# Cutting the weight blocks of a fused hybrid block into their two fp32r parts in two halves, while recurrences run

## The chip, the cores and the metric

The kernel runs on one core of a Trainium2 chip. The metric is the device time of one execution in microseconds, median over the runs shown. The core has TensorE (PE, matmuls and transposes, with its weight loads listed apart as PEld), VectorE (DVE), ScalarE (ACT), GpSimd (POOL) and SyncE (SP), which issues the DMAs of the weights. The engines run side by side, each in its own order, and wait for one another by semaphores.

## The reference

The block takes 256 tokens and 16 meta tokens in front of them, width 2048, in fp32. One input projection gives the inputs of three recurrences and of three gates:

```python
h = jnp.concatenate([meta, x], axis=1)                  # 272 x 2048
xn = rmsnorm(h, norm_g[l])
(a_q, ..., g_a, g_b, g_c) = split_cols(xn @ w_in[l])    # w_in: 2048 x 18568
y_a = hgrn2_mixer(a_q, a_f, a_i, a_z, ...)              # A: 8 heads of 128 x 128
y_b = mlstm_mixer(b_q, b_k, b_v, b_o, b_ig, b_fg, b_z, ...)   # B: 4 heads
y_c = rwkv7_mixer(c_r, c_k, c_v, c_wd, c_ad, c_z, ...)  # C: 16 heads of 64 x 64
merged = (jax.nn.sigmoid(g_a) * (y_a @ w_br[l, 0])
          + jax.nn.sigmoid(g_b) * (y_b @ w_br[l, 1])
          + jax.nn.sigmoid(g_c) * (y_c @ w_br[l, 2]))
h = h + merged @ w_out[l]
return rmsnorm(h, final_norm_g)[:, N_META:]
```

Each recurrence goes over the tokens in chunks and carries a state from one chunk to the next. C solves a triangular system in each chunk.

## The kernel before

**Products.** Every large product is made of three matmuls in fp32r, a rounded form of fp32: with x = xH + xL and w = wh + wl, where the H and h parts are the rounded values and the L and l parts what is left, the kernel sums xH·wh, xL·wh and xH·wl. The parts of the activations are made once. The parts of the weights are made as the weights arrive.

**The weight stream.** `Stream` (its `cut` is the function that the change edits) brings the weights in 372 units of 128 partitions. A unit is 4 x 256 elements (four k tiles of 128 rows, 256 columns) in the first part of the run, 2 x 512 in the gates and the end, and 4 x 128 for four units at the start. `load` issues the unit's DMA into `raw` (4 buffers). `cut` makes two instructions: ACT copies `raw` into `wh`, which rounds it, and DVE subtracts `wh` from `raw` into `wl`; each has 3 buffers. `next` hands the oldest pair to the products. A unit feeds 24 matmuls that write PSUM tiles called `gp` (12 of 512 columns in the gates). In `unit`, the 24 go through one column tile of 128 and then the other; in each, k runs from 0 to 3 and each k has its three matmuls.

**What runs when.** The program first normalizes and transposes x (tiles `xt`, then `xH` and `xL`), then takes the projection column block by column block: groups b0, c1, b1, c2, a0, a1, c3, a2, a3, with c0 first, then the gates of B, C and A with their products with `w_br`, then `w_out`. The recurrence of a group is a generator. `Order` keeps a clock for each engine by a list of prices; after the matmuls of a column tile `pump` lets a generator go on if its next step would be ready by those clocks. The prices are taken from every DVE and ACT instruction that is written, through the helper `Priced`, whose line 127 therefore stands in the profile for all of them (matmuls are on line 186, transposes on line 193). After that the tile framework's scheduler sets the order of each engine's queue, so the order in the code isn't the order on the engines. The steps of a generator that the profile names are these. For A: `aE`, `aW`, `aQ`, `aK` (decays and their products), `ATT` (scores), `avt` (values), `aY`, `aYH`, `aYL` (output norm), all in PSUM tiles called `bank`. For C, in PSUM tiles called `cbank`: `BK` and `RA` (inputs of the chunks), `SC` (scores), `LU`, `LV`, `Ltmp` and `LT` (the triangular solve, a row of DVE instructions for a whole group), then for each of five chunks `UV,SC`, `cX,Vm`, `UV,BT` and `SC,UV`, `RA,Zs`, each needing the one before, and at the end `cSH`, `cSL` (the norm of the group's output).

**The end of the last C recurrence.** `l_setup`, called ahead of the first gate block, closes the pool of C when its last recurrence has ended, and opens the pool `late`, which holds among others the tiles `yHB` and `yLB` (the parts of B's output) of the block after it. The matmuls of the first gate block itself (8 units) read only `xH`, `xL` and the weights. `x_again`, after the last block of gate B, sets `late["rp"]`.

Of the kernel before, what the change touches and what calls it, by code (L numbers as in the profile page):

```python
# [9 lines left out]
F32 = mybir.dt.float32  # L10
# [4 lines left out]
ALU = mybir.AluOpType  # L15
# [135 lines left out]
def kernel(  # L151
# [29 lines left out]
    od = Order()  # L181
    V = Priced(nc.vector, "dve", od, tc)
    S = Priced(nc.scalar, "act", od, tc)
# [148 lines left out]
    class Stream:  # L332
# [18 lines left out]
        def cut(self):  # L351
            if not self.raw:
                return
            raw, uk, m = self.raw.pop(0)
            if self.extra and len(self.todo) + len(self.raw) < len(self.extra):
                h, l = self.extra.pop(0)
            else:
                h = wts.tile([P, uk, max(m, 256)], F32R, name="wh", tag="wh", bufs=3)
                l = wts.tile([P, uk, max(m, 256)], F32R, name="wl", tag="wl", bufs=3)
            saved, od.ready = od.ready, 0.0  # L360
            S.copy(out=h[:, :, 0:m], in_=raw[:, :, 0:m])
            od.ready = 0.0
            V.tensor_tensor(out=l[:, :, 0:m], in0=raw[:, :, 0:m], in1=h[:, :, 0:m].bitcast(F32), op=ALU.subtract)
            od.ready = saved
            self.split.append((h, l))

        def next(self):
# [4 lines left out]
                self.load()  # L372
            return self.split.pop(0)

    ws = Stream()

    def unit(h, l, u, kts, ps, aH, aL, t0, n, js):
# [955 lines left out]

    late = {}
    WB = 512
    TK = 2

# [222 lines left out]
    for u in range(KT // UK):  # L1562
        h, l = ws.next()
        unit(h, l, u, KT, gw[0][:, 0:T], xH, xL, 0, T, slice(0, P))
        h, l = ws.next()
# [103 lines left out]
    for n, (c0, m) in enumerate(outs):  # L1669
        ps = [gps.tile([P, 512], F32, name="gp", tag="g") for _ in range(2)]  # L1670
        us = KT * m // 1024
        if n < len(outs) - 1:
            for u in range(us):
                h, l = ws.next()
# [55 lines left out]
```

## Time and profile before

| | before |
|---|---|
| time, median of 3 runs | 1229.77 us (1229.72 to 1230.2) |
| the profiled execution's own time | 1229.33 us |
| its span | 1227.6 us |
| TensorE busy | 1208.1 us, 98% |
| VectorE busy | 879.2 us, 72% |
| ScalarE busy | 665.0 us, 54% |
| HBM read | 202.19 MB, 168 GB/s over the span |

The span runs from the first to the last instruction that the profile counts. The busy times are sums over the whole of it and include stages with different limits. A matmul counts as busy until its result is written, and matmuls overlap, so that their durations don't add up to the time that a row of them takes; that is read from their starts.

### The profile page before, as it was taken

How to read it: one execution, taken by the hardware profiler on the slowest of the kernel's cores; microseconds unless marked ns; L12 is line 12 of the kernel's file. 1: busy time of each engine (PE TensorE's matmuls, PEld its weight loads, DVE VectorE, ACT ScalarE, POOL GpSimd, SP SyncE). 2: the span in 40 equal slices, each digit the busy share in tenths (PEclk: the TensorE clock that was granted, in tenths of full speed). 3: DMA queues.
4: the chain of work that ended last, by engine and by line, in shares of the span. 5: the costliest groups of instructions: out<-in, count | busy, mean ns of one | idle time of the engine just before them, and what ended most of it. 6: DMA issues, size and time to landing. Idle time of an engine off the chain costs nothing.

```text
span 1227.6 us, 23061 instructions
## 1 busy us (share of the span) xinstructions
PE 1208.1 (98%) x9224; PEld 1104.2 (90%) x9224; DVE 879.2 (72%) x1491; ACT 665.0 (54%) x1032; POOL 57.0 (5%) x167
## 2 busy tenths in 40 slices
PE   8999999999999999999999999999999999999997
PEld 8999999999999999999999988888888888888887
DVE  6688996697975889995889986644555565556554
ACT  6765455663445764766664657544444444445444
POOL 3100001000051000010000000000000000000000
PEclk9999999999999999999999999999999999999999
DMA  8645564465563554463554454666766676665663
GB/s 254 184 138 166 155 172 130 129 183 155 155 171 104 158 165 137 140 170 105 162 163 142 139 164 153 190 188 189 226 197 193 191 225 200 191 193 172 193 197 121
DMA packets 172996, 207.43 MB, mean 169 GB/s; under 512 B 22331, under 2 KB 127160, under 8 KB 172488
## 3 DMA queue, kind: packets, MB, share of 16 engines
q1 hardware_dynamic: 171688, 202.21, 56.2%
q0 software_dynamic: 880, 3.22, 0.8%
q8 instruction: 72, 1.18, 0.4%
q10 hardware_dynamic: 320, 0.53, 0.1%
q14 instruction: 36, 0.29, 0.1%
HBM read 202.19 MB, written 3.74 MB: 168 GB/s over the span
## 4 chain that ended last, share of the span: by engine, by line
PE 85%; DVE 9%; ACT 3%; issue 2%; POOL 0%; DVEq 0%; ACTq 0%; POOLq 0%
PE gp L186 76%; PE cbank L186 5%; DVE wl L127 3%; PE bank L186 3%; ACT wh L127 1%; DVE Ltmp L127 1%; PE cbank L193 1%; DVE LV L127 1%; PE bank L193 1%; DVE UV L127 0%; DVE aY L127 0%; ACT L127 0%; DVE BK L127 0%; DVE aW L127 0%; DVE SC L127 0%
## 5 line engine op out<-in xcount | busy, mean ns | idle before, releaser
L127 DVE TENSOR_TENSOR wl<-raw,wh 128x1024 fp32r<-128x1024 f32 (+1 forms) x370 | 449.3, 1215 | 243.6 <-ACT wh L127 242.2
L127 ACT CAST wh<-raw 128x1024 fp32r<-128x1024 f32 (+1 forms) x370 | 386.7, 1046 | 387.0 <-PE gp L186 352.4
L186 PE MATMUL gp<-xH,wh 128*128 128x272 f32 (+3 forms) x1552 | 448.1, 289 | 0.2 <-ACT xH L127 0.2
L186 PE MATMUL gp<-xH,wl 128*128 128x272 f32 (+3 forms) x1552 | 444.0, 286 | 1.6 <-DVE wl L127 1.6
L186 PE MATMUL gp<-xL,wh 128*128 128x272 f32 (+3 forms) x1552 | 443.8, 286 | 0.1
L186 PEld LDWEIGHTS gp<-xH,wl 128*128 128x128 f32 x1552 | 292.4, 188 | 2.9 <-DVE wl L127 2.6
L186 PEld LDWEIGHTS gp<-xH,wh 128*128 128x128 f32 x1552 | 292.5, 188 | 2.2 <-ACT xH L127 0.5
L186 PEld LDWEIGHTS gp<-xL,wh 128*128 128x128 f32 x1552 | 292.2, 188 | 0.9 <-DVE xL L127 0.3
L186 PE MATMUL gp<-wh,xH 128*128 128x512 f32 x384 | 150.6, 392 | 0.0
L186 PE MATMUL gp<-wh,xL 128*128 128x512 f32 x384 | 150.5, 392 | 0.0
L186 PE MATMUL gp<-wl,xH 128*128 128x512 f32 x384 | 150.3, 391 | 0.0
L186 PEld LDWEIGHTS gp<-wh,xL 128*128 128x128 f32 x384 | 72.1, 188 | 15.5
L186 PEld LDWEIGHTS gp<-wl,xH 128*128 128x128 f32 x384 | 72.2, 188 | 15.0
L186 PEld LDWEIGHTS gp<-wh,xH 128*128 128x128 f32 x384 | 72.1, 188 | 15.0
L186 PE MATMUL gp<-wh,mH 128*128 128x512 f32 (+1 forms) x144 | 51.1, 355 | 0.0
L186 PE MATMUL gp<-wh,mL 128*128 128x512 f32 (+1 forms) x144 | 50.9, 354 | 0.0
L186 PE MATMUL gp<-wl,mH 128*128 128x512 f32 (+1 forms) x144 | 50.9, 354 | 0.0
L127 DVE TENSOR_TENSOR LV<-LV,Ltmp 40x31 f32<-40x31 f32 (+15 forms) x124 | 41.0, 331 | 2.6
L127 DVE TENSOR_TENSOR Ltmp<-LU,LV 40x31 f32<-40x31 f32 (+15 forms) x124 | 41.1, 332 | 2.4
L186 PEld LDWEIGHTS gp<-wh,mL 128*128 128x128 f32 x144 | 27.2, 189 | 3.8
L186 PEld LDWEIGHTS gp<-wh,mH 128*128 128x128 f32 x144 | 27.2, 189 | 3.7
L186 PEld LDWEIGHTS gp<-wl,mH 128*128 128x128 f32 x144 | 27.2, 189 | 3.7
(420 smaller groups left out, 1476.0 us busy)
## 6 DMA issues: line engine op xcount, KB each, us to landing
raw<-in_w_in_dram SPq DMA_DIRECT2D x288, 512.0 KB, 3.7
raw<-in_w_br_dram SPq DMA_DIRECT2D x48, 512.0 KB, 4.2
raw<-in_w_out_dram SPq DMA_DIRECT2D x32, 512.0 KB, 3.6
hres<-in_x_dram POOLq DMA_DIRECT2D x2, 1024.0 KB, 5.9
xt<-in_x_dram SPq DMA_DIRECT2D x3, 512.0 KB, 5.0
raw<-in_w_in_dram SPq DMA_DIRECT2D x4, 256.0 KB
fg<-in_final_norm_g_dram POOLq DMA_DIRECT2D x1, 1024.0 KB, 5.1
scr<-SC SPq DMA_DIRECT2D x16, 40.0 KB, 1.7
```

What stands on the lines that cost most here:

```text
L127: r = f(*a, **k)
L186: nc.tensor.matmul(o, lhsT, rhs, start=start, stop=stop)
L193: nc.tensor.transpose(o, a, i)
```

## The change

`cut` makes the two parts of a unit in two halves, k tiles 0 and 1 first, then 2 and 3 (for a unit of 2 x 512: k tile 0, then 1). Each half is a copy on ACT and a subtract on DVE. A unit with fewer than 1024 columns in all stays whole (the four of 4 x 128), and so does every unit that is cut after `x_again` has set `late["rp"]`. `late` is created earlier in the program, since `cut` now looks into it. The tiles and their buffers are the same, and so are the DMAs and the matmuls.

```diff
@@ -358,9 +358,14 @@
             saved, od.ready = od.ready, 0.0
-            S.copy(out=h[:, :, 0:m], in_=raw[:, :, 0:m])
-            od.ready = 0.0
-            V.tensor_tensor(out=l[:, :, 0:m], in0=raw[:, :, 0:m], in1=h[:, :, 0:m].bitcast(F32), op=ALU.subtract)
+
+            n = 1 if uk * m < 1024 or "rp" in late else 2
+            for i in range(n):
+                us = slice(i * uk // n, (i + 1) * uk // n)
+                od.ready = 0.0
+                S.copy(out=h[:, us, 0:m], in_=raw[:, us, 0:m])
+                od.ready = 0.0
+                V.tensor_tensor(out=l[:, us, 0:m], in0=raw[:, us, 0:m], in1=h[:, us, 0:m].bitcast(F32), op=ALU.subtract)
             od.ready = saved
@@ -372,6 +377,7 @@
+    late = {}
     ws = Stream()
@@ -1333,7 +1339,6 @@
-    late = {}
     WB = 512
```

In the built program 238 units are cut in two: VectorE's queue has 476 subtracts of 512 elements and 130 of 1024, where it had 368 of 1024. `Order` prices the halves (0.07 and 0.12 us a piece more), and the scheduler sees other instructions, so rows move on every engine. Three places follow, each as it stands in the engine's queue.

The first is VectorE in the stretch where group 2 of C is solved while a recurrence of A runs. `wl` rows are the cuts, `Ltmp`, `LV` and `LT` the solve, `aE`, `aQb`, `aKb` and `aW` steps of A. Before:

```order
L127 TENSOR_TENSOR wl<-raw,wh 128x1024
L127 TENSOR_TENSOR Ltmp<-LU,LV 40x31
L127 TENSOR_TENSOR aQb<-aQ,aG 128x272
L127 TENSOR_TENSOR LV<-LV,Ltmp 40x31
L127 TENSOR_TENSOR aKb<-aKb,aK 128x272
L127 TENSOR_TENSOR aE<-aC 128x2x8x16 x2
L127 COPY LT<-LV 20x1024
L127 TENSOR_TENSOR wl<-raw,wh 128x1024
L127 TENSOR_TENSOR aW_6772<-aE,aK 128x2x8x16
```

After the change the same steps of A stand here:

```order
L127 TENSOR_TENSOR aQb<-aQ,aG 128x272
L127 TENSOR_TENSOR aKb<-aKb,aK 128x272
L127 TENSOR_TENSOR aE<-aC 128x2x8x16 x2
L127 TENSOR_TENSOR wl<-raw,wh 128x512 x2
L127 TENSOR_TENSOR Ltmp<-LU,LV 40x135
L127 TENSOR_TENSOR wl<-raw,wh 128x512
L127 TENSOR_TENSOR LV<-LV,Ltmp 40x5x27
L127 TENSOR_TENSOR wl<-raw,wh 128x512
L127 TENSOR_TENSOR Ltmp<-LU,LV 40x112
L127 TENSOR_TENSOR aW_7024<-aE,aK 128x2x8x16
```

The solve, which had come to its last row (31 elements) beside these steps of A, is now at 135, with five pairs of rows still to come, and its end has moved behind them. Two whole units are cut between `aE` and `aW`, where before it was one.

The second place is TensorE at the end of the last C recurrence, around `cSL`. `bank` rows are steps of A, `gp` rows with `xH` or `xL` belong to the first gate block. Before:

```order
L186 MATMUL cbank<-RA,Zs 64x16 x2
L186 MATMUL bank<-aQ_9906,aK_9879 64x64 x2
L186 MATMUL bank<-aQ_9921,aK_9897 128x144
L186 MATMUL bank<-aQR,aK_9897 128x16
L186 MATMUL bank<-aQ_9921,aK_9897 128x144
L186 MATMUL bank<-aQR,aK_9897 128x16
L186 MATMUL gp<-wh,xH 128x512
L186 MATMUL gp<-wl,xH 128x512
L186 MATMUL gp<-wh,xL 128x512
L186 MATMUL gp<-wh,xH 128x512
```

Four more rows of the gate block stand between these and `cSL,bonesR`. After the change:

```order
L186 MATMUL bank<-ATT,avt 128x144
L186 MATMUL cbank<-SC,UV 64x16 x2
L186 MATMUL cbank<-RA,Zs 64x16 x2
L186 MATMUL cbank<-SC,UV 64x16 x2
L186 MATMUL cbank<-RA,Zs 64x16 x2
L186 MATMUL bank<-aAT_5721,avt_10473 128x16
L186 MATMUL cbank<-cSL,bonesR 128x256
L186 MATMUL cbank<-cSH,bonesR 128x256
L186 MATMUL cbank<-cSL,bonesR 128x256
L186 MATMUL cbank<-cSH,bonesR 128x256
L186 MATMUL gp<-wh,yHB 128x512
```

The rows of the gate block are all ahead of this place now; one row of A of 16 columns is left between the last `RA,Zs` and `cSL`, and the block after follows `cSH` at once.

The third place is TensorE's beginning, where the second weight unit meets the transposes of `xt`. Before:

```order
L186 MATMUL gp<-xH,wh 128x272
L186 MATMUL gp<-xL,wh 128x272
L193 MATMUL bank<-ident,xt_88 128x128
L186 MATMUL gp<-xH,wl 128x272
L186 MATMUL gp<-xH,wh 128x272
```

After the change:

```order
L186 MATMUL gp<-xL,wh 128x272
L186 MATMUL gp<-xH,wl 128x272
L193 MATMUL bank<-ident,xt_88 128x128
L193 MATMUL cbank<-ident,xt_88 128x128
L193 MATMUL bank<-ident,xt_88 128x128
```

The transpose that stood ahead of the unit's first matmul with `wl` stands behind four of them now.

## Rows read from the trace of the kernel before

**Rows 1.** The page, busy times: us, share of the span, instructions.

```profile
PE 1208.1 (98%) x9224; PEld 1104.2 (90%) x9224; DVE 879.2 (72%) x1491; ACT 665.0 (54%) x1032; POOL 57.0 (5%) x167
```

**Rows 2.** The page, the chain that ended last, by engine and line.

```profile
PE gp L186 76%; PE cbank L186 5%; DVE wl L127 3%; PE bank L186 3%; ACT wh L127 1%; DVE Ltmp L127 1%; PE cbank L193 1%; DVE LV L127 1%; PE bank L193 1%; DVE UV L127 0%; DVE aY L127 0%; ACT L127 0%; DVE BK L127 0%; DVE aW L127 0%; DVE SC L127 0%
```

**Rows 3.** Windows: us, busy time and instructions of each engine, granted clock, DMA.

```profile
450.00:530.00 80.00, 78.09 (x807) 76.24 (x806) 75.40 (x171) 46.52 (x77) 0.32 (x2) 1.00 0.53 147
...
640.00:710.00 70.00, 67.56 (x722) 66.20 (x721) 66.77 (x150) 41.83 (x70) 0.13 (x1) 1.00 0.52 143
```

**Rows 4.** Groups by shape: count | busy us, mean ns | idle before, releasers.

```profile
L127 DVE TENSOR_TENSOR wl<-raw,wh 128x1024 fp32r<-128x1024 f32 x366 | 446.6, 1221 | 243.5 <-ACT wh L127 242.1
...
L127 DVE TENSOR_TENSOR wl<-raw,wh 128x512 fp32r<-128x512 f32 x4 | 2.8, 688 | 0.2 <-ACT wh L127 0.2
...
L127 ACT CAST wh<-raw 128x1024 fp32r<-128x1024 f32 x366 | 384.3, 1050 | 387.0 <-PE gp L186 352.4 <-issue 22.3 <-DVE bdn L127 2.9
...
L127 ACT CAST wh<-raw 128x512 fp32r<-128x512 f32 x4 | 2.5, 626 | 0.0
```

**Rows 5.** TensorE's waits: us in total, times, longest us.

```profile
PE bank L186 <- DVE aW L127: 1.6, 2, 1.0
PE gp L186 <- DVE wl L127: 1.6, 4, 0.7
...
PE cbank L186 <- DVE SC L127: 1.5, 4, 0.6
...
PE cbank L186 <- ACT cX L127: 0.9, 3, 0.3
PE cbank L186 <- DVE UV L127: 0.5, 1, 0.5
PE cbank L186 <- ACT UV L127: 0.4, 1, 0.4
```

**Rows 6.** Timeline of VectorE in the first full stretch: start us, us.

```profile
504.22 1.21 DVE L127 TENSOR_TENSOR wl<-raw,wh 128x1024 fp32r<-128x1024 f32 x1
505.36 0.37 DVE L127 TENSOR_TENSOR Ltmp<-LU,LV 40x220 f32<-40x220 f32 x1
...
506.07 0.68 DVE L127 TENSOR_TENSOR aYL<-aY,aYH 128x512 fp32r<-128x512 f32 x1
506.67 0.36 DVE L127 TENSOR_TENSOR Ltmp<-LU,LV 40x207 f32<-40x207 f32 x1
```

**Rows 7.** Timeline at the start, VectorE and TensorE: start us, us.

```profile
17.14 1.83 DVE L127 TENSOR_TENSOR wl<-raw,wh 128x1024 fp32r<-128x1024 f32 x2 [0.37 <-ACT wh L127]
...
18.31 0.33 PE L193 MATMUL bank<-ident,xt 128*128 128x128 f32 x1 [0.37 <-ACT xt L127]
```

**Rows 8.** Timeline of the first full stretch, VectorE and TensorE.

```profile
489.42 1.21 DVE L127 TENSOR_TENSOR wl<-raw,wh 128x1024 fp32r<-128x1024 f32 x1
...
490.68 0.39 PE L186 MATMUL gp<-xH,wl 128*128 128x256 f32 x1
...
520.39 0.39 PE L186 MATMUL gp<-xH,wl 128*128 128x256 f32 x1 [0.44 <-DVE wl L127]
...
521.21 0.28 PE L186 MATMUL gp<-xH,wl 128*128 128x256 f32 x1
```

**Rows 9.** Timeline of the last chain of C, TensorE, then VectorE.

```profile
741.47 0.45 PE L186 MATMUL cbank<-UV,BT 128*64 128x64 f32 x8
...
743.34 0.60 PE L186 MATMUL cbank<-UV,SC 128*128 128x128 f32 x4
...
744.72 0.62 PE L186 MATMUL cbank<-cX,Vm 128*128 128x64 f32 x4
...
746.06 0.23 PE L186 MATMUL cbank<-SC,UV 128*64 128x16 f32 x1
...
749.91 0.28 PE L186 MATMUL cbank<-cSL,bonesR 128*128 128x256 f32 x1
...
748.62 0.69 DVE L127 TENSOR_TENSOR cSL<-cSq,cSH 128x512 fp32r<-128x512 f32 x1 [0.36 <-ACT cSH L127]
```

## The prediction

> **What bounds the kernel now.** I read the page's busy line first: TensorE (PE) is busy 98% of the span, VectorE (DVE) 72%, ScalarE (ACT) 54% [rows 1]. The chain that ended last says the same: matmuls into `gp` are 76% of it, and cuts are the next engine's part, `wl` with 3% of the span and `wh` with 1%, together near 50 us [rows 2]. Those 50 us are no bill for the change: the chain passes through a cut wherever it set the order, and the list of TensorE's own waits is the better count. There `wl` stopped TensorE four times, for 1.6 us in all, `aW` for 1.6, `SC` for 1.5, `cX` and `UV` for 1.8 [rows 5]. So what can be won is a few microseconds of 1229, spread over named places, and what can be lost depends on where DVE has no time to spare. [...] Elsewhere DVE stands 10 to 40% idle.
>
> The grouped lines then show how a cut is paced. DVE sat idle 243.5 us ahead of `wl` rows, waiting for ACT's `wh`; ACT sat idle 387.0 us ahead of `wh`, 352.4 of them until a TensorE matmul had ended, which is the release of a `wh` buffer [rows 4]. In most of the run, then, the cut is early and waits for TensorE, not the other way round. The halves write into the same whole tile, so the first half waits for the same release as the whole cut did, and no buffer comes free earlier.
>
> **The change, part by part.** A measurement of this kernel tells 0.2% from no change, 2.5 us, and the profiled execution took 1229.33 us, 0.44 below the median of the runs. I make the sum against the profiled one and add 0.4.
>
> *The extra instructions.* 238 units are cut in two, so DVE gets 238 more subtracts and ACT 238 more copies. By durations alone one `wl` of 1024 takes 1221 ns and two of 512 take 2 x 688, 155 ns more; on ACT it is 2 x 626 against 1050, 202 ns more [rows 4]. But independent instructions start before the one ahead has ended: the `wl` at 504.22 lasts 1.21 us and the next row starts 1.14 after it; the 512-wide `aYL` at 506.07 lasts 0.68 and the next starts 0.60 after it [rows 6]. By starts the price is 2 x 0.60 - 1.14 = 0.06 us. Bounds: 0.06 to 0.155 us per unit on DVE, 14 to 37 us in all; I take 0.1, since the half rows are neighboured now by half rows and now by others. Outside the two full stretches it is covered by the idle time of DVE and costs nothing; ACT has 46% idle time and no full stretch, so its extra is covered too. Inside them lie 42 units (22 and 20 `wl` rows), 2.5 to 6.5 us of DVE work against 4.6 and 3.2 us idle.
>
> [...]
>
> *What first halves give.* The matmuls of a unit go k by k through one column tile, three rows each, and then through the next. The first that needs half two (k = 2) comes six rows behind the first with `wl`: 0.82 us, 520.39 to 521.21 [rows 8]. A unit whose `wl` is late may begin when half one is there, some 0.6 us sooner, and half two, 0.6 later, is then in time. All four waits on `wl` (1.6 us) are of this kind; the one that ended at 520.39 took 0.44 us [rows 5, 8].
>
> *Full stretches, the net.* The price list and the framework's scheduler move instructions too. I added up DVE's rows along both orders, with the start-to-start times above. In the first stretch the DVE work ahead of the cut around the 137th unit is up to 2.1 us later, seen from TensorE's place, among others because steps of A and of the solve (`LV`, `Ltmp`) end 1.5 to 2.5 units later than before. Before, that cut ended at 490.63 and its first matmul came at 490.68, so there is no slack to take the delay [rows 8]. Less 0.65 for the first half, less some 0.2 that the `aW` waits give back since TensorE comes to `aW` later: +1.2 (0 to +4). In the second stretch the largest such delay, 2.1 us again, meets a TensorE that comes 0.42 of a unit later (24 rows, of which six took 0.82 us with a restart in them, so some 2.9 us a unit, and 1.2 us): 2.1 - 0.65 - 1.2, +0.3 (-1 to +3).
>
> *Small waits elsewhere.* A row of a recurrence that stands behind a cut waits for at most a half of it. The four waits on `SC` (1.5 us) stand behind a `wl` of 1.21 us; behind one of 0.69 up to 0.53 each is gone [rows 4, 5]; I take 0.3 each, -1.2 (0 to -1.5). The waits on `cX` and `UV` behind `wh` on ACT lose at most 1.05 - 0.63 = 0.42 each [rows 4]; with 0.2 for four of them, -0.8 (0 to -1.2). *The start:* TensorE stood until 18.31 because transposes of `xt` were queued ahead of the matmuls with the second `wl`, which ran as the first of two from 17.14 and was over some 1.2 us later [rows 4, 7]. In the new order the transposes stand behind these matmuls, and half a `wl` is there by about 17.4: -0.5 (0 to -0.5).
>
> *The last chain of C.* This is the largest loss that I see. The five chunks of C's last group form a chain that runs on every latency: `UV,BT` to `UV,SC` took 1.87 us, `UV,SC` to `cX,Vm` 1.38, `cX,Vm` to `SC,UV` 1.34, and from the last `SC,UV` at 746.06 `cSL` was ready only at 748.62 + 0.69 = 749.31, 3.2 us later [rows 9]. Before, 76 matmuls of the first gate block lay between the rows of this chain, by the engine's order, and filled them, so that TensorE waited there only twice, 0.4 us for `UV` and 0.3 or less for `cX` [rows 5]. The next block needs `yH`, which lives in the pool opened when C's scan has ended, so only these eight units can be filler. In the new order the chain starts four units later (the solve of group 3 ends 5 units later on DVE), and only 38 of the matmuls are left: from `UV,BT` of the third chunk on there are three. What remains as cover are steps of A, `aV` transposes and `ATT,avt`. Step by step: about 0.45 open at `UV,SC` twice, 0.35 at `cX,Vm`, 0.2 at `SC,UV`, and at the end 3.2 less 0.6 of the `SC,UV` and `RA,Zs` rows less what the scheduler still finds: 2.3. Together 3.4 against 1.1 of waits and their slower restarts before: +2.3 (+1 to +4).
>
> *Sum:* -0.5 - 1.2 - 0.8 + 1.2 + 0.3 + 2.3 = +1.3, so 1230.6 against the profiled execution and **1231.0** against the median.
>
> **Rivals.** *Faster.* The halves do all they can: waits on `SC`, `cX`, `UV`, `wl` and the one at the start are gone (1.5 + 1.2 + 1.6 + 0.5 = 4.8), and the chain's end is covered as before. 1229.8 - 4.8 = 1225.0; with a tail of +2.3, 1227.3. For it: each of these waits stands behind a whole cut. Against: the filler of the tail is gone by the order, which is fixed. It decides at whether TensorE is so late at the chain that `cSL` is there when it asks. Chance 0.26.
>
> *Slower.* In the full stretches DVE is the bound. At 0.155 us a unit, 42 units give 6.5 us; with 2 us of it covered by idle time and first halves, and the tail at +3 less 1.5 of small gains, +6: 1236. For it: 95% busy and a slack of 0.05 us at 490.68 [rows 3, 8]. It decides from the point at which a half two ends more than 0.82 us behind the first `wl` matmul of its unit. [...] Chance 0.27.
>
> *Nothing.* The second half follows the first at once on both engines, waits of TensorE go by other chains (`aW`, `aYL`, `cX`), and the tail is filled by steps of A: 1229.8. Chance 0.07.
>
> **The numbers.** My forecast has 0.40, with its own range 1228.5 to 1233.5; a quarter of it lies above 1232.2, the rest within 0.2%. That gives faster 0.26, same 0.37, slower 0.37. The range reaches to both rivals' cores, 1225.0 to 1237, and leaves about 2 in 10 outside.
>
> **What would show it.** Mean `wl` of 512 near 690 ns, and starts 0.60 apart; idle time of ACT before `wh` still put down to TensorE. Waits on `SC` under 0.6 in all; no `xt` wait near 18. In the gate block, waits of 2 us or more on `cSL` just ahead of the first `yHB` matmul. In the two stretches DVE's busy share at 97% or more and `wl` waits of 1 to 3 us. I am wrong if TensorE has no wait of over a microsecond at `cSL`, or if `wl` waits pass 4 us.

## The result, and the profile after

The changed kernel took 1237.72 us (1237.45 to 1238.77, 4 runs), the one before in the same session 1229.74 us: a ratio of 1.0069, 95% interval 1.0051 to 1.0086. It is slower by 8.0 us. The forecast was 1231.0 and the range ended at 1237.

The page's busy times and the chain, which answer to [rows 1, 2], show how little such totals say here. TensorE is busy 98% as before, and `wl` has a smaller share of the chain than it had.

```profile
PE 1210.7 (98%) x9224; PEld 1105.0 (89%) x9224; DVE 891.9 (72%) x1729; ACT 685.3 (55%) x1270; POOL 52.8 (4%) x167
...
PE gp L186 77%; PE cbank L186 5%; PE bank L186 3%; DVE wl L127 2%; ACT wh L127 1%; PE cbank L193 1%; DMA raw<-in_w_in_dram 1%; DMA xt<-in_x_dram 1%; PE bank L193 1%; DVE aW L127 0%; DVE Ltmp L127 0%; DVE aE L127 0%; DVE LV L127 0%; DMA raw<-in_w_out_dram 0%; DVE aM L127 0%
```

The list of TensorE's waits says more (us in total, times, longest). Against [rows 5], `SC` has gone from 1.5 us to 0.8, where the forecast had under 0.6, and `UV` is gone, as forecast; `wl` has gone from 1.6 to 5.1, over the 4 us that the prediction named as a sign of being wrong, and `aW` from 1.6 to 2.7; and there are waits that the kernel before did not have, on `cSL`, `cY` and `prm`, and a larger one on `ZT`.

```profile
PE gp L186 <- DVE wl L127: 5.1, 6, 1.6
PE bank L186 <- DVE aW L127: 2.7, 4, 0.9
PE cbank L186 <- DVE cSL L127: 2.5, 1, 2.5
...
PE cbank L186 <- ACT cX L127: 1.2, 4, 0.5
PE cbank L186 <- ACT ZT L127: 1.0, 2, 0.8
PE gp L193 <- DVE prm L127: 1.0, 1, 1.0
PE cbank L186 <- ACT cY L127: 1.0, 1, 1.0
PE cbank L186 <- DVE SC L127: 0.8, 1, 0.8
```

Five of the six waits on `wl`, 4.85 us of the 5.1, lie in the two full stretches, 450 to 530 and 640 to 710 us. The three longest, in the timeline of TensorE:

```profile
520.30 0.38 PE L186 MATMUL gp<-xH,wl 128*128 128x256 f32 x1 [1.01 <-DVE wl L127]
...
667.15 0.39 PE L186 MATMUL gp<-xH,wl 128*128 128x272 f32 x1 [1.59 <-DVE wl L127]
...
700.88 0.39 PE L186 MATMUL gp<-xH,wl 128*128 128x272 f32 x1 [1.31 <-DVE wl L127]
```

To see where the 8 us arise, time alone does not serve, since the two kernels have done different work at the same moment. I took for each matmul its start less the sum of the usual start-to-start times of all TensorE rows ahead of it (by shape, the 30th percentile of the kernel before), which is TensorE's lost time so far, and compared it in the middle of the same weight unit. After minus before, in us (the times are those of the changed kernel):

| in unit | after | old prices (below) |
|---|---|---|
| 30 | 0.0 | -0.1 |
| 130 (468 us) | -2.3 | -1.7 |
| 160 (592 us) | -0.7 | -2.3 |
| 195 (714 us) | +0.5 | -2.4 |
| 215 (796 us) | +8.2 | -2.3 |
| end | +8.6 | -2.2 |

Up to unit 130 the change won 2.3 us. The two stretches with recurrence A took 2.8, and the 80 us around the last chain of C took 7.7. The end took 0.4.

The timeline of TensorE in that last chain shows three things: a wait of 0.96 us at `UV,SC`, one of 2.52 us at `cSL`, and behind it matmuls of the next block 0.43 us apart, which from 765.87 on are 0.23 apart.

```profile
755.47 0.68 PE L186 MATMUL cbank<-UV,SC 128*128 128x128 f32 x4 [0.96 <-ACT cY L127]
...
759.00 0.40 PE L186 MATMUL bank<-aAT,avt 128*128 128x16 f32 x2
761.90 0.36 PE L186 MATMUL cbank<-cSL,bonesR 128*128 128x256 f32 x1 [2.52 <-DVE cSL L127]
...
763.05 0.63 PE L186 MATMUL gp<-wl,yHB 128*128 128x512 f32 x1
763.47 0.63 PE L186 MATMUL gp<-wh,yHB 128*128 128x512 f32 x1
...
765.61 0.42 PE L186 MATMUL gp<-wl,yHB 128*128 128x512 f32 x1
765.87 0.40 PE L186 MATMUL gp<-wh,yLB 128*128 128x512 f32 x1
766.10 0.40 PE L186 MATMUL gp<-wh,yHB 128*128 128x512 f32 x1
```

The windows explain the third. The columns are those of [rows 3]; behind the busy times stands the granted clock. It was 0.56 and 0.59 from 762 to 766 (0.50 from 763 to 765), after 2 us in which TensorE had done next to nothing, and 1.00 from 766 to 768. The first two rows answer to [rows 3]: in the full stretches VectorE was *less* busy than before, 74.17 and 62.14 us against 75.40 and 66.77.

```profile
450.00:530.00 80.00, 77.02 (x797) 75.15 (x797) 74.17 (x186) 47.66 (x97) 0.32 (x2) 1.00 0.51 145
640.00:710.00 70.00, 66.46 (x711) 64.57 (x710) 62.14 (x157) 40.69 (x86) 0.13 (x1) 1.00 0.47 131
...
760.00:762.00 2.00, 0.10 (x1) 0.13 (x2) 0.69 (x1) 2.00 (x5) 0.00 (x0) 1.00 0.00 0
762.00:764.00 2.00, 2.00 (x8) 1.71 (x9) 1.29 (x2) 1.68 (x5) 0.00 (x0) 0.56 0.05 8
764.00:766.00 2.00, 2.00 (x7) 1.57 (x6) 1.48 (x3) 1.71 (x4) 0.00 (x0) 0.59 0.00 0
766.00:768.00 2.00, 2.00 (x11) 1.61 (x10) 0.86 (x2) 1.01 (x2) 0.57 (x1) 1.00 0.30 66
```

One more window bears on the argument. The prediction has VectorE idle for 10 to 40% outside the two stretches, but from 300 to 350 us it was busy 48.51 of 50 us before, 97%. TensorE was busy for all 50.00 us there, before and after the change, so in this third full stretch the halves cost it nothing. Before, then after:

```profile
300.00:350.00 50.00, 50.00 (x412) 49.68 (x412) 48.51 (x105) 22.86 (x36) 1.90 (x10) 1.00 0.58 166
...
300.00:350.00 50.00, 50.00 (x413) 49.79 (x412) 48.78 (x121) 25.01 (x52) 2.21 (x12) 1.00 0.59 169
```

The grouped lines and a timeline of VectorE give the price of a half. By durations two halves take 2 x 683 - 1221 = 145 ns more than a whole [rows 4]; two in a row took 1.28 us from the first's start to the second's end, where a whole takes 1.21 (over the 152 such pairs of this trace the median is 1.29).

```profile
L127 DVE TENSOR_TENSOR wl<-raw,wh 128x512 fp32r<-128x512 f32 x480 | 315.6, 683 | 81.0 <-ACT wh L127 76.8 <-PE gp L186 2.2
L127 DVE TENSOR_TENSOR wl<-raw,wh 128x1024 fp32r<-128x1024 f32 x128 | 156.7, 1224 | 156.4 <-ACT wh L127 156.4
```

```profile
719.02 1.28 DVE L127 TENSOR_TENSOR wl<-raw,wh 128x512 fp32r<-128x512 f32 x2
720.23 0.78 DVE L127 TENSOR_TENSOR aE<-aC 128x272 f32<-128x272 f32 x2
```

### The profile page after: what moved, and what is told of

Read it like the earlier page. It is cut to its first block, busy times and chain, and to the rows that moved or that the text cites. A ratio compares the mean times of both kernels' runs of the same rounds, so it can differ in the third digit from the quotient of the medians.

```text
span 1236.2 us, 23549 instructions
## 1 busy us (share of the span) xinstructions
PE 1210.7 (98%) x9224; PEld 1105.0 (89%) x9224; DVE 891.9 (72%) x1729; ACT 685.3 (55%) x1270; POOL 52.8 (4%) x167
## 4 chain that ended last, share of the span: by engine, by line
PE 85%; DVE 7%; ACT 4%; DMA 2%; issue 1%; SPq 0%; ACTq 0%; DVEq 0%
PE gp L186 77%; PE cbank L186 5%; PE bank L186 3%; DVE wl L127 2%; ACT wh L127 1%; PE cbank L193 1%; DMA raw<-in_w_in_dram 1%; DMA xt<-in_x_dram 1%; PE bank L193 1%; DVE aW L127 0%; DVE Ltmp L127 0%; DVE aE L127 0%; DVE LV L127 0%; DMA raw<-in_w_out_dram 0%; DVE aM L127 0%
## 5 line engine op out<-in xcount | busy, mean ns | idle before, releaser
L127 DVE TENSOR_TENSOR wl<-raw,wh 128x512 fp32r<-128x512 f32 (+1 forms) x608 | 472.3, 797 | 237.4 <-ACT wh L127 233.2
L127 ACT CAST wh<-raw 128x512 fp32r<-128x512 f32 (+1 forms) x608 | 413.9, 709 | 374.7 <-PE gp L186 326.7
```

The costliest lines, as they stand in the source:

```text
L127: r = f(*a, **k)
```

## The experiments

Two theories stood against each other. **P**: the loss comes from the planner, that is `Order` with its prices. Charged for two instructions a unit instead of one, it lets the recurrences' steps go later, and the last chain of C runs out of matmuls to hide behind. **S**: the extra instructions themselves cost, where VectorE is full. The change can be taken apart along just this line, since what `cut` issues and what `Order` is charged are two things. "Filler" below is the number of weight matmuls in TensorE's queue between the first step of the last chain of C (`Vm,ZT`) and its `cSL`: 76 before, 38 after.

**Halves, charged as whole cuts** (split_old_prices).

```diff
+            was = dict(od.clk)
             for i in range(n):
...
+            if n == 2:
+                od.clk = was
+                od.ready = 0.0
+                od.cost("act", 0.12 + 0.84e-3 * uk * m)
+                od.ready = 0.0
+                od.cost("dve", 0.07 + 1.05e-3 * uk * m)
             od.ready = saved
```

> All 238 units are cut in halves as in the change, but the planner is charged the price of a whole cut, so that the last chain of C has 76 matmuls of the gate block as filler again instead of 38. Theory P (the loss comes from the planner's prices, which push the last chain of C behind its filler): the 6.7 us of the tail are gone, 1229 to 1231 us, no wait on cSL over 1 us. Theory S (the extra instructions themselves cost, in the stretches where VectorE is full): the 238 extra subtracts are still there, 1234 us or more, and the waits on wl stay near 5 us.

Measured: 1226.88 us, ratio to before 0.998 (0.9972 to 0.9989). All 476 half subtracts are still there, and the kernel is not only rid of the 8 us but faster than the one before, by more than P had expected. Its list of waits has no `cSL`, and `wl` costs 1.4 us:

```profile
PE cbank L186 <- DVE SC L127: 1.5, 3, 1.0
PE bank L186 <- DVE aW L127: 1.4, 3, 0.7
PE gp L186 <- DVE wl L127: 1.4, 5, 0.4
```

The full stretches, in its windows, hold more VectorE work than before, and TensorE stands less in them: it is busy for 78.58 and 68.67 us against 78.09 and 67.56 [rows 3]:

```profile
450.00:530.00 80.00, 78.58 (x902) 76.78 (x902) 75.67 (x191) 48.64 (x101) 0.32 (x2) 1.00 0.55 153
640.00:710.00 70.00, 68.67 (x823) 66.96 (x821) 68.25 (x172) 43.03 (x89) 0.13 (x1) 1.00 0.52 144
```

**Whole cuts, charged as halves** (whole_new_prices), the other half of the change alone.

```diff
             n = 1 if uk * m < 1024 or "rp" in late else 2
-            for i in range(n):
-                us = slice(i * uk // n, (i + 1) * uk // n)
-                od.ready = 0.0
-                S.copy(out=h[:, us, 0:m], in_=raw[:, us, 0:m])
-                od.ready = 0.0
-                V.tensor_tensor(out=l[:, us, 0:m], in0=raw[:, us, 0:m], in1=h[:, us, 0:m].bitcast(F32), op=ALU.subtract)
+            was = dict(od.clk)
+            S.copy(out=h[:, :, 0:m], in_=raw[:, :, 0:m])
+            od.ready = 0.0
+            V.tensor_tensor(out=l[:, :, 0:m], in0=raw[:, :, 0:m], in1=h[:, :, 0:m].bitcast(F32), op=ALU.subtract)
+            od.clk = was
+            for i in range(n):
+                od.ready = 0.0
+                od.cost("act", 0.12 + 0.84e-3 * uk * m / n)
+                od.ready = 0.0
+                od.cost("dve", 0.07 + 1.05e-3 * uk * m / n)
```

> No unit is cut in halves; only the planner is charged as if it were (two prices for each of the 238 units). The last chain of C then has 40 matmuls of filler. Theory P: the loss is there without a single extra instruction, 1235 to 1238 us, with a wait of 2 us or more on cSL and matmuls at the lower clock behind it. Theory S: nothing is added on VectorE, so 1229 to 1231 us.

Measured: 1241.98 us, ratio 1.0103 (1.0089 to 1.0117), slower still than the change. No instruction is added, and the waits of the change are there:

```profile
PE gp L186 <- DVE wl L127: 4.8, 6, 1.6
PE cbank L186 <- ACT ZT L127: 2.3, 2, 1.5
PE cbank L186 <- DVE cSL L127: 2.1, 1, 2.1
```

The time is also 4 us above what P gave. By lost time against the kernel before, 2.1 us are gone at unit 30 and 5.5 at unit 195, and the last chain takes 8.0: the prices cost time in other places than the chain too.

With these two S has fallen: prices alone cost 13 us (1228.95 was the kernel before in these runs), halves alone win 2.1.

**Halves for the first 130 units** (split_first_130).

```diff
-            n = 1 if uk * m < 1024 or "rp" in late else 2
+            self.count = getattr(self, "count", 0) + 1
+            n = 2 if uk * m >= 1024 and self.count <= 130 else 1
```

> Halves for the first 130 units only, prices accordingly; the last chain of C has its 76 matmuls. Theory P: the changed kernel was 2.3 us ahead of the one before at unit 130 by TensorE's work done, and nothing behind it is changed, so 1227.0 to 1228.0 us. Theory S: the full stretches lie behind unit 130, so no loss there either, but no gain: 1229.7 us.

Measured: 1230.04 us, ratio 1.001 (1.0001 to 1.0019). A miss for P; the figure of S, 1229.7, was nearer, but not for its reason. By lost time it was 2.4 us ahead at unit 130, as expected, and level again at unit 160; its waits on `wl` are 4.0 us in all, the longest 1.5. "Nothing behind it is changed" was wrong: from 468 to 594 us only 152 of VectorE's 220 rows stand in the order that they had before, though every cut there is whole; from 594 to 715 all 230 do. That the higher charges, which the planner's clocks carry over, move the steps of the next stretch fits this; the clocks themselves were not followed.

**Filler for the wait at `cSL`** (tail_fill). The changed kernel, with matmuls whose result is overwritten:

```diff
         ps = cbank()
+        for i in range(20 if g == 3 else 0):
+            tc.keep_in_program_order(nc.tensor.matmul(ps[:, 0:256], bonesR, xH[:, i % KT, 0:256], start=True, stop=True))
         for j in range(2):
```

> The changed kernel with 20 added fp32r matmuls of 256 columns on TensorE just ahead of the last cSL product (they write the PSUM tile that the product then overwrites), some 2.4 us of work in the 2.5 us wait. If the granted clock fell because TensorE stood idle in that wait, it stays at 1.00 now and the first gate-B branch matmuls come 0.233 us apart instead of 0.43: 1.5 us less, 1236.2 us. If the clock falls for another reason, or those matmuls are slow through their data, the time stays at 1237.7 us.

Measured: 1235.27 us, ratio to before 1.0049 (1.0036 to 1.0061), 2.45 less than the change, and 1.7 less when each is taken against the kernel before of its own session. In its timeline the 20 matmuls fill the wait, and the matmuls of the next block are 0.23 us apart from the first:

```profile
758.64 2.62 PE L803 MATMUL cbank<-xH,bonesR 128*128 128x256 f32 x20
...
761.47 0.39 PE L186 MATMUL cbank<-cSL,bonesR 128*128 128x256 f32 x1
...
762.05 0.39 PE L186 MATMUL gp<-wh,yHB 128*128 128x512 f32 x1
762.28 0.40 PE L186 MATMUL gp<-wl,yHB 128*128 128x512 f32 x1
```

The granted clock of those windows is 1.00:

```profile
759.00:761.00 2.00, 2.00 (x20) 2.00 (x19) 0.28 (x1) 1.99 (x4) 0.00 (x0) 1.00 0.00 0
761.00:763.00 2.00, 1.92 (x14) 1.64 (x13) 1.65 (x3) 1.95 (x5) 0.00 (x0) 1.00 0.03 8
763.00:765.00 2.00, 2.00 (x10) 1.67 (x9) 1.15 (x3) 2.00 (x4) 0.00 (x0) 1.00 0.00 0
```

So the fall of the clock in the tail came from TensorE's idleness and cost about 1.6 us: in unit 215 this kernel stands at 793.8 us and the change at 795.8, of which 0.4 was there before the tail. The rest of the difference lies at the run's end. The mean granted clock over the whole span is 0.995 or 0.996 in the four executions of the change and 0.997 or 0.998 in the five of this kernel. That TensorE works through the wait does not shorten the wait.

Not every wait is followed by a lower clock, and its length alone does not decide. In the trace of price_dve_only, below, TensorE waited 1.56 us until 544.54 and 2.88 us until 666.30. Behind the shorter wait the clock fell to 0.67 and 0.50, behind the longer one it stayed at 1.00:

```profile
666.30 0.40 PE L186 MATMUL gp<-xH,wl 128*128 128x272 f32 x1 [2.88 <-DVE wl L127]
...
545.00:547.00 2.00, 2.00 (x13) 1.86 (x12) 1.64 (x6) 1.06 (x4) 0.00 (x0) 0.67 0.31 52
547.00:549.00 2.00, 2.00 (x21) 1.80 (x21) 1.11 (x3) 1.70 (x5) 0.56 (x3) 0.50 0.61 212
667.00:669.00 2.00, 2.00 (x18) 2.00 (x17) 2.00 (x7) 1.08 (x4) 0.00 (x0) 1.00 0.20 17
```

**One price at a time** (price_act_only, price_dve_only): as split_old_prices, but with two prices on one of the two clocks, for VectorE:

```diff
-                od.cost("dve", 0.07 + 1.05e-3 * uk * m)
+                for i in range(n):
+                    od.ready = 0.0
+                    od.cost("dve", 0.07 + 1.05e-3 * uk * m / n)
```

> All 238 units in halves; the planner is charged two prices on ScalarE's clock (0.12 us more a unit) and the whole price on VectorE's. The last chain of C has 55 matmuls of filler, against 76 with the old prices (1226.9 us) and 38 in the change (1237.7). If the tail's filler sets the time, whichever price moved it, the time lies between in proportion: 1226.9 + 10.8 x 21/38 = 1232.9 us, within 2. If one price alone does the harm and it is ScalarE's, 1237; if it is VectorE's, 1227.

> The counterpart: two prices on VectorE's clock (0.07 us more a unit), the whole price on ScalarE's. 43 matmuls of filler are left in the last chain of C. By the filler 1226.9 + 10.8 x 33/38 = 1236.3 us, within 2. If ScalarE's price alone does the harm, 1227.

Measured: 1232.03 us (ratio 1.0023, 1.0012 to 1.0035) and 1235.5 us (1.0047, 1.0032 to 1.0062). Both within 1 us of what the filler gave. Neither price alone is to blame; each costs a part.

**A price nearer to the measured one** (price_measured): VectorE's charge for the pair is `0.13 + 1.05e-3 * uk * m`, 0.06 over the whole cut.

> All 238 units in halves; the planner is charged on VectorE the whole price and 0.06 us, which is about what two halves in a row take longer than one whole in the trace of the changed kernel (1.28 against 1.21), and the whole price on ScalarE. 56 matmuls of filler in the last chain. If each matmul missing there costs 0.28 us, as between 76 (1226.9), 55 (1232.0), 43 (1235.5) and 38 (1237.7): 1226.9 + 0.28 x 20 = 1232.5 us, within 2, though the price is the truer one. If a true price plans best, 1227 or less.

Measured: 1233.03 us, ratio 1.0025 (1.0015 to 1.0035). That is within 0.6 of what the filler gave, and a truer price plans worse than the whole cut's.

**Prices under the whole cut's** (price_less_010, price_less_020): the same line with -0.03 and -0.13 in place of 0.13.

> Halves, with VectorE's price for the cut 0.10 us under the whole cut's. The last chain of C begins 2.7 units earlier than in the kernel before and has 120 matmuls of filler. At 76 the waits of the chain were about 1 us, so the rule of 0.28 us a matmul ends there: at most 1 us is won in the tail, and steps planned too early may wait elsewhere: 1225.5 to 1229 us. If the rule went on, 1215 us.

> The same with 0.20 us less, 134 matmuls of filler. The tail wins nothing more; steps that the planner takes to be ready sooner than they are make TensorE wait in the full stretches: 1227 to 1232 us.

Measured: 1234.44 us (ratio 1.0049, 1.0035 to 1.0063) and 1236.7 us (1.0066, 1.0049 to 1.0083). Both worse than expected. In the trace of the first, the tail loses nothing any more (7.6 us of lost time more than before in unit 195, 7.7 in 215), but elsewhere TensorE waits longer for steps of A and C than with the old prices (`aW` 3.5 us against 1.4, `SC` 2.9 against 1.5), as it would if they were placed too early:

```profile
PE bank L186 <- DVE aW L127: 3.5, 4, 1.2
PE cbank L186 <- DVE SC L127: 2.9, 3, 1.2
PE cbank L186 <- DVE UV L127: 2.3, 2, 1.2
```

That execution took 1237.05 us, 2.6 over the median of its kernel, and in its windows the granted clock was 0.50 from 634 to 636, so not all of its 7.7 us is the usual cost of these prices.

Over the kernels with halves that differ in their prices alone, the lost time from unit 195 to 215 against the filler reads: 134 matmuls, -0.8 us; 120 and 76 (old prices), 0.1 each; 56, 4.5; 55, 4.2; 43, 6.3; 38, 7.7; and with whole cuts and 40, 8.0. This is an agreement over eight kernels; no run changed the filler and left the rest of the plan as it was.

**Four pieces** (quarters_old_prices): `n = 4` for units of 4 x 256, old prices.

> Units of 4 x 256 in four pieces instead of two, charged as whole cuts; 72 matmuls of filler in the last chain. Pieces of 256 start some 0.34 us apart where they follow one another (other rows of that width), so four cost about 0.2 us more than one whole. In the 42 units of the full stretches that is 6 to 9 us of added VectorE work over the halves' 2.5. If added work in the full stretches is paid in full, 1233 to 1236 us; if idle time and earlier first matmuls cover it, as with halves, 1226 to 1229 us.

Measured: 1232.78 us, ratio 1.0032 (1.0017 to 1.0046), at the edge of what full payment gave. But by lost time only 2.7 of the 5.7 us lost against halves arise in the two full stretches; 2.6 are lost by 446 us, before the first begins. Waits on `SC` are 4.3 us, at 114, 279, 451 and 633 us, and behind the first the granted clock was 0.58 and 0.56 from 116 to 120. Which rows of quarters the waits stand behind was not followed further.

**Whole cuts in the full stretches** (skip_full_old_prices): as split_old_prices, with

```diff
+            self.count = getattr(self, "count", 0) + 1
+            full = 132 <= self.count <= 149 or 180 <= self.count <= 196
-            n = 1 if uk * m < 1024 or "rp" in late else 2
+            n = 1 if uk * m < 1024 or full or "rp" in late else 2
```

> Halves with old prices, but whole cuts for units 132 to 149 and 180 to 196 (the two stretches in which VectorE is full). 71 matmuls of filler. If halves cost time where VectorE is full, this is faster than halves everywhere: 1225 us or less. If they gain there too, since TensorE may begin a late unit on its first half, it is slower: 1228 to 1230 us.

Measured: 1228.28 us, ratio 0.999 (0.9981 to 0.9999). The edit spares 35 of the 42 units. The halves do not lose where VectorE is full; the difference of 1.4 us to halves everywhere (0.8 when each is taken against the kernel before of its own session) has the sign of a gain, but the intervals of the two overlap.

**Halves to the end of the run** (all_old_prices): without the condition on `"rp"`.

> Halves for every unit up to the end of the run, gates and output product too, with old prices; the last chain is that of the halves with old prices (1226.9 us). After the last recurrence VectorE is idle about 45% of the time and TensorE waits once for a cut, near the end, for 0.3 us or less: 1226.9 us, within 1. If the extra instructions cost time by themselves, 130 more of them add 4 us or more.

Measured: 1227.96 us, ratio 0.9988 (0.9979 to 0.9997). That is 1.1 over the expected time, and the same as split_old_prices within their intervals; where VectorE is idle 130 more pairs cost nothing that can be seen.

## Why the prediction was wrong

- *The small waits and the start* had -2.5 in the sum. Three of the four waits on `SC` and two of those on `cX` lie ahead of unit 130, which with the start makes -1.8 up to there. Measured: -2.3. The size is near; the start's part of it isn't. The 0.7 us won until 18.7 us were given back between 26.6 and 31.3, in a wait of 0.44 on `xL` at 27.43 among others. The wait on `SC` behind unit 130, which I had shrinking as well, grew from 0.37 to 0.83 us.
- *The full stretches, the net* had +1.5, bounds -1 to +7. Measured: +2.8, so in the bounds, but for a wrong reason. I held VectorE's fullness for the cause and asked for 97% busy. It was 93 and 89% busy in the change, and with old prices 95 and 98%, without the loss; and the window from 300 to 350, 97% busy, I had counted as 10 to 40% idle. `wl` waits in the two stretches are 4.85 us in the change, where I had 1 to 3, and 1.4 with old prices. What costs is the place that the planner gives the steps, not the price of a half. That price came out near the 0.06 us that I had from the starts: two halves in a row took 0.07 us more than a whole (1.28 against 1.21), where the durations give 0.145 and I had taken 0.1.
- *The last chain of C* is the step that failed: "+2.3 (+1 to +4)". Measured: +7.7. Its parts as I gave them, 0.45 twice, 0.35, 0.2 and 2.3, add up to 3.75 and not to 3.4, which would have made it +2.65. The mechanism was right, that the chain starts later and 38 matmuls of filler are left, and the profile shows the wait at `cSL` just ahead of the first `yHB` matmul that I named. Its size was off in three places. The wait at `cSL` was 2.5 us and a slower restart, 2.75 in all, for 2.3. A step of A ahead of the chain and the chain's beginning and middle waited as well: `aW` 0.47, `ZT` 0.78, `cX` 0.40 and `UV,SC` 0.96 (3.5 with the restarts and a second, small wait on `cX`), where I had 1.1 for the later steps and nothing at the beginning. And the clock, 1.00 in the two stretches [rows 3] and no part of my sum, fell behind the wait: 1.5 us, since seven matmuls of 0.43 us took the place of seven of 0.23, and the four rows of `cSL` and `cSH` were slow too (0.72 us, against 0.58 in tail_fill). That is 2.75 + 3.5 - 1.0 (before) + 1.5 = 6.7 of the 7.7. The last 1.0 us is not resolved to single waits.
- *The sum*: the terms measured are -2.3 + 2.8 + 7.7 + 0.4 = 8.6 for the profiled execution, where I had +1.3. The rival "slower" gave the tail +3 and would have had 1236, near the time measured, but by a mechanism, VectorE's fullness, that the runs refute: as a number it is luck.
- That the price list itself, and not the instructions, moves the tail was visible ahead of the result in the order of the two kernels, and I named it, but did not weigh it as a part of the change that can be had or left apart.
- *The signs*: the mean of 683 ns for a half, starts 0.60 us apart, no wait on `xt` near 18 and a wait of over 2 us at `cSL` came as I named them. Waits on `SC` under 0.6 us and VectorE at 97% in the two stretches did not, and `wl` waits passed 4 us, which I had named as a sign of being wrong.

## What to carry to other kernels

When a planner places work by a price list, an edit has two effects, on the engines and on the plan, and they can have opposite signs: here the halves won 2.1 us, and their prices cost 10 on top of them (8.0 over the kernel before instead of 2.1 under it). Take them apart by charging the old price for the new work, and the new price for the old work, before judging the edit. And count what is left to hide a serial chain behind: a chain that has lost its filler shows its latency as waits (2.5 us at `cSL` with 38 matmuls, none there with 76), and a wait behind which the clock falls is paid a second time (1.5 us here). More filler is not the aim by itself: with 120 and 134 matmuls the tail lost nothing, and the kernels still took 1234.44 and 1236.7 us.

## What the runs showed of the hardware

A wait of 2.5 us on TensorE in the middle of the changed kernel's run was followed by a granted clock of 0.56 to 0.59 in the next 4 us, and 20 matmuls in the wait kept it at 1.00 (tail_fill). In another run (price_dve_only) it fell behind a wait of 1.56 us, to 0.67 and 0.50, and stayed at 1.00 behind one of 2.88 us. Two independent VectorE subtracts of 512 fp32 elements cost 0.07 us more than one of 1024 where they follow each other, half of what their durations (683 and 1224 ns) say.
